# High and low activations side by side: 512-column matmuls in the weight-stationary products of a three-way split float32 decoder

## The chip, the cores and the metric

The kernel runs on one core of one Trainium2 chip. The time of a run is the device time of one execution in microseconds (us); the time before is the median of three runs. The profile is of one further execution, which has its own time. TensorE is PE in the profile (its weight loads are PEld), VectorE is DVE, ScalarE is ACT, GpSimd is POOL, SyncE is SP.

## The reference, cut to what matters

Four layers over 256 tokens of 1,024 features. Each layer has a mixer (layers 0 and 3 a convolution module, layer 1 a state-space mixer, layer 2 differential attention), then cross-attention to 256 memory tokens with 4 heads, then a gated feed-forward of inner width 2,816; each ends in a layer norm.

```
for i in range(DEPTH):
    y = conformer_conv(...) | ssd_mixer(...) | diff_attention(...)
    x = post_norm(x, y, ln_g[i, 0], ln_b[i, 0])
    x = post_norm(x, memory_cross_attention(x, mem, xa_w_q[i], xa_w_kv[i], xa_w_out[i]), ...)
    x = post_norm(x, swiglu(x, ff_w_in[i], ff_w_out[i]), ...)

def post_norm(x, y, g, b):
    return layer_norm(DN_ALPHA * x + y, g, b)

def swiglu(x, w_in, w_out):
    g, u = jnp.split(x @ w_in, 2, axis=-1)
    return (jax.nn.silu(g) * u) @ w_out
```

Everything is float32.

## The kernel before

**Split products.** Each float32 operand is held as a high part h (rounded to the type that TensorE multiplies) and a low part l, the rest. A product a·b is the sum of three matmuls into the same PSUM bank: ah·bh, ah·bl, al·bh (`mm3`, lines 199, 200 and 201).

**Weights.** `_Weights` streams blocks of 128 x 1024 numbers (512 KB) from HBM in a fixed plan: a DMA from SP's queue into one of four raw buffers, a cast on ACT to the high part `wh` (L152), two subtractions of 128x512 on DVE to the low part `wl` (L155). The pairs lie in a ring of seven; the block three ahead of the one taken is prepared when a block is taken. A cast into a ring place must wait until the block that lay there has been used.

**Activations.** `transpose_split` turns the 256 tokens into `XTh` and `XTl`, two tiles of 128 x 8 x 256 (eight k-tiles of features, 256 tokens); `MTh` and `MTl` are the same for the memory.

**The two forms of product.** In `gemm_a` and in the output products the weights are the moving operand, 512 columns per matmul. In `gemm_b_steps` the weights are stationary and the tokens move, 256 columns per matmul: for 256 output features (two halves j of 128) and 1,024 input features in two weight blocks b of four k-tiles,

```
for b in range(2):
    wh, wl = self.W.get(name, i, 4 * b, 4, *segs)
    for k in range(4):
        kk = 4 * b + k
        for j in range(2):
            self.mm3(ps[:, j, :], wh[:, k, js], wl[:, k, js], xh[:, kk, :], xl[:, kk, :], ...)
```

That is 24 matmuls of 256 columns per block and 48 per product. Both halves j share one PSUM bank. `gemm_b` serves three places: `ff`, the loop over feed-forward chunks 1 to 10 (a gate product and an up product in each); `q_part` in the cross-attention (heads 2 and 3); and the four K units per layer of `kv_unit`, which project the memory for the next cross-attention and are laid by `kv_unit` and its generator between other work.

**PSUM.** Eight banks: four for output sums (`pso`), two for the products above and other middle results (`psi`, taken in turn), two for transposes and scores (`psm`).

**A feed-forward chunk.** Gate product into one psi bank, tanh on ACT (L726), gate times sigmoid on DVE (L727, reads PSUM), up product into the other psi bank, product on DVE (L733, reads PSUM), split into `ch` and `cl` (L206, L210). Then two output blocks of 12 matmuls of 512 columns for the chunk before (L290, L291, L294). `out_tail` ends the layer with 48 output matmuls, the layer norm of both token halves (x0, x1; L334, L242, L341, L346) and the transposes into the next XT (L219), among which a K unit of the memory runs.

The order of instructions on each engine is set when the program is recorded; a scheduler in the recording layer places them by estimated readiness.

Of the kernel before, what the change touches and what calls it, by code (L numbers as in the profile page):

```python
# [26 lines left out]
D_FF = 2816  # L27
# [136 lines left out]
class _Trunk:  # L164
# [97 lines left out]
    def gemm_b(self, *args):  # L262
        for _ in self.gemm_b_steps(*args):
            pass

    def gemm_a(self, name, i, segs, done, which="o"):
# [50 lines left out]

    def new_xt(self, wanted=True):

        self.XTh = self.XTl = None  # L320
        if wanted:
            self.XTh = self.main.tile([P, KT, S], F32R, tag="XTh", name=self.uid("XTh"))
            self.XTl = self.main.tile([P, KT, S], F32R, tag="XTl", name=self.uid("XTl"))
# [31 lines left out]
    def setup(self):  # L355
        nc, ins = self.nc, self.ins
        self.x = [self.main.tile([P, D], F32, tag=f"x{t}", name=f"x{t}") for t in range(T)]
        self.alpha = ALPHA
        self.ident = self.const.tile([P, P], F32, name="ident")
        nc.vector.memset(self.ident, 1.0)  # L360
        nc.gpsimd.affine_select(
            out=self.ident, in_=self.ident, pattern=[[-1, P]], compare_op=ALU.is_equal, fill=0.0, base=0,
            channel_multiplier=1,
        )
        self.mhalf = self.const.tile([P, 8], F32, name="mhalf")
        nc.vector.memset(self.mhalf, -0.5)
        self.new_xt()
        self.MTh = self.main.tile([P, KT, S], F32R, name="MTh")
        self.MTl = self.main.tile([P, KT, S], F32R, name="MTl")
        self.memK = self.main.tile([P, KT, S], F32, name="memK")  # L370
        self.memVh = self.main.tile([P, T, D], F32R, name="memVh")
        self.memVl = self.main.tile([P, T, D], F32R, name="memVl")
        early = self.const.tile([P, 1], F32, name="early")
        nc.scalar.activation(out=early, in_=self.mhalf[:, 0:1], func=AF.Tanh)
        for t in range(T):
            for c in range(2):
                cs = slice(c * 512, (c + 1) * 512)
                nc.sync.dma_start(out=self.x[t][:, cs], in_=ins["x"][0][t * P : (t + 1) * P, cs])
            with self.tc.high_priority():
                self.transpose_split(self.x[t], self.XTh, self.XTl, t)  # L380
            if t == 0:
                self.W.prefetch(1)
# [8 lines left out]
    def kv_steps(self, layer):  # L391
# [3 lines left out]
        self.kv_next += 1  # L395
        i, u = divmod(u, 8)
        nc = self.nc
        ps = self.bank("i", a=2)
        if u < 4:
            yield from self.gemm_b_steps(ps, "xa_w_kv", i, ((u * 256, 256),), self.MTh, self.MTl)  # L400
            nc.scalar.copy(out=self.memK[:, 2 * u : 2 * u + 2, :], in_=ps)
            return
# [180 lines left out]
    def xattn(self, i):  # L583
        nc = self.nc
        ln = self.load_ln(i, 1)
        with self.stage_pool(f"xa{i}", 2) as wk:
# [17 lines left out]
                return (qh[:, 0:2, :], ql[:, 0:2, :]), (qh[:, 2:4, :], ql[:, 2:4, :])  # L604

            def q_part(h):
                ps = self.bank("i", a=2)
                self.gemm_b(ps, "xa_w_q", i, ((h * 256, 256),), self.XTh, self.XTl)
                qh, ql = parts(2, "xr")
                self.split(ps, qh, ql, 1.0 / 16.0)  # L610
                return qh, ql

            def s_part(h, q):
# [78 lines left out]
    def ff(self, i, nxt, hooks):  # L692
        nc = self.nc
        ln = self.load_ln(i, 2)
        with self.stage_pool(f"ff{i}", 2) as wk:
# [20 lines left out]
            for c in range(1, NFF):  # L716
                for step in hooks.get(c, ()):
                    step()
                psg = self.bank("i")
                psu = self.bank("i")  # L720
                self.gemm_b(
                    psg.rearrange("p (a b) -> p a b", a=2), "ff_w_in", i, ((c * 256, 256),), self.XTh, self.XTl
                )
                th = wk.tile([P, 512], F32, tag="fth", name=self.uid("fth"))
                sg = wk.tile([P, 512], F32, tag="fsg", name=self.uid("fsg"))
                nc.scalar.activation(out=th, in_=psg, func=AF.Tanh, scale=0.5)  # L726
                nc.vector.scalar_tensor_tensor(out=sg, in0=th, scalar=1.0, in1=psg, op0=ALU.add, op1=ALU.mult)  # L727
                self.gemm_b(
                    psu.rearrange("p (a b) -> p a b", a=2), "ff_w_in", i, ((D_FF + c * 256, 256),),
                    self.XTh, self.XTl,  # L730
                )
                h2 = wk.tile([P, 512], F32, tag="fh2", name=self.uid("fh2"))
# [673 lines left out]
```

## Time and profile before

| what | value |
|---|---|
| median of three runs | 1762.99 us (1761.61 to 1763.95) |
| profiled execution | 1762.06 us, its span 1760.3 us |
| granted TensorE clock, mean | 0.996 of full speed |
| PE busy | 1718.8 us, 98% of the span, 11,356 matmuls |
| PE weight loads | 1555.8 us, 88% |
| DVE busy | 1247.9 us, 71% |
| ACT busy | 844.6 us, 48% |
| DMA | 55.9% of 16 engines, 176 GB/s |

The span is the time from the first to the last instruction that the profile shows. Busy matmul time counts overlapping matmuls once; the duration of a single matmul (about 0.28 us for 256 columns) holds its pipeline, so what one costs in a row is the distance of starts.

### The profile page before, as it was taken

To read this page: it belongs to the slowest core of one execution; us is meant where nothing else is said; L and a number is where in the kernel's file an instruction comes from. 1 tells how busy PE (TensorE), PEld (TensorE's weight loads), DVE (VectorE), ACT (ScalarE), POOL (GpSimd) and SP (SyncE) were. 2 spreads that over 40 slices of the span, in tenths; PEclk is the share of its full clock that TensorE was granted. 3 is DMA by queue.
4 is the path that set the end of the run, shared out by engine and by line. 5 is a ranking of instruction groups with operands and counts; after the bars stand their busy time and mean duration, and the time that the engine had idled before them with its cause. 6 is when DMAs were issued, how large, how long until landed. Compare 5 with 4: busy or idle time off the path is not lost.

```text
span 1760.3 us, 29243 instructions
## 1 busy us (share of the span) xinstructions
PE 1718.8 (98%) x11356; PEld 1555.8 (88%) x11356; DVE 1247.9 (71%) x2306; ACT 844.6 (48%) x1250; POOL 55.6 (3%) x72
## 2 busy tenths in 40 slices
PE   7999999999999999999999999999999999999998
PEld 4887989999999998999998889889899888879997
DVE  4879675557898878675557677775555889775555
ACT  3445444444665654454444565544444445544442
POOL 0000000000011010000000000000000000000000
PEclk9999999999999999999999999999999999999999
DMA  7637465656656645465655643556565645556562
GB/s 229 210 115 224 148 198 185 187 185 183 202 169 179 179 157 167 138 211 184 191 181 183 188 132 120 181 155 207 170 187 183 217 139 170 190 169 189 182 190 72
DMA packets 234098, 310.05 MB, mean 176 GB/s; under 512 B 14104, under 2 KB 196774, under 8 KB 233960
## 3 DMA queue, kind: packets, MB, share of 16 engines
q1 hardware_dynamic: 233832, 307.90, 55.9%
q8 instruction: 89, 1.46, 0.3%
q14 instruction: 49, 0.40, 0.1%
q10 hardware_dynamic: 128, 0.29, 0.0%
HBM read 307.07 MB, written 1.08 MB: 175 GB/s over the span
## 4 chain that ended last, share of the span: by engine, by line
PE 72%; DVE 9%; DMA 5%; ACT 2%; issue 2%; SPq 0%; POOL 0%; DVEq 0%; ACTq 0%; POOLq 0%
PE psi L199 14%; PE psi L200 14%; PE psi L201 14%; PE pso L291 5%; PE pso L290 5%; PE pso L294 5%; DVE wl L155 3%; PE pso L199 2%; PE pso L201 2%; PE pso L200 2%; DMA raw<-in_xa_w_q 2%; ACT wh L152 1%; DVE st L242 1%; DVE x L334 1%; DVE x L346 1%
## 5 line engine op out<-in xcount | busy, mean ns | idle before, releaser
L155 DVE TENSOR_TENSOR wl<-raw,wh 128x512 fp32r<-128x512 f32 x1074 | 704.3, 686 | 396.8 <-ACT wh L152 394.5
L152 ACT CAST wh<-raw 128x1024 fp32r<-128x1024 f32 x537 | 560.3, 1048 | 686.6 <-PE psi L200 312.9
L199 PE MATMUL psi<-XTh,wh 128*128 128x256 f32 x1792 | 510.4, 285 | 0.2
L200 PE MATMUL psi<-XTl,wh 128*128 128x256 f32 x1792 | 507.9, 283 | 0.0
L201 PE MATMUL psi<-XTh,wl 128*128 128x256 f32 x1792 | 507.7, 283 | 0.0
L199 PEld LDWEIGHTS psi<-XTh,wh 128*128 128x128 f32 x1792 | 344.4, 192 | 3.9 <-issue 2.0
L200 PEld LDWEIGHTS psi<-XTl,wh 128*128 128x128 f32 x1792 | 344.5, 192 | 2.5 <-issue 0.8
L201 PEld LDWEIGHTS psi<-XTh,wl 128*128 128x128 f32 x1792 | 344.4, 192 | 0.0
L290 PE MATMUL pso<-wh,ch 128*128 128x512 f32 x448 | 176.1, 393 | 0.0
L291 PE MATMUL pso<-wl,ch 128*128 128x512 f32 x448 | 175.3, 391 | 0.0
L294 PE MATMUL pso<-wh,cl 128*128 128x512 f32 x448 | 139.4, 391 | 0.0
L294 PEld LDWEIGHTS pso<-wh,cl 128*128 128x128 f32 x448 | 84.1, 188 | 17.7
L291 PEld LDWEIGHTS pso<-wl,ch 128*128 128x128 f32 x448 | 84.4, 188 | 15.6
L290 PEld LDWEIGHTS pso<-wh,ch 128*128 128x128 f32 x448 | 84.4, 188 | 15.4 <-ACT ch L206 0.2
L199 PE MATMUL pso<-wh,XTh 128*128 128x512 f32 x224 | 89.5, 400 | 0.5 <-ACT XTh L206 0.4
L201 PE MATMUL pso<-wh,XTl 128*128 128x512 f32 x224 | 88.9, 397 | 0.3 <-DVE XTl L208 0.2
L200 PE MATMUL pso<-wl,XTh 128*128 128x512 f32 x224 | 87.7, 392 | 0.0
L234 POOL TENSOR_TENSOR rs<-rv,mhalf 128x1 f32<-128x1 f32 (+2 forms) x40 | 37.0, 924 | 1330.5 <-DVE rv L233 1330.5
L199 PE MATMUL pso<-wh,ch 128*128 128x512 f32 x192 | 76.0, 397 | 0.0
L201 PE MATMUL pso<-wh,cl 128*128 128x512 f32 x192 | 74.6, 392 | 0.0
L200 PE MATMUL pso<-wl,ch 128*128 128x512 f32 x192 | 74.4, 391 | 0.0
L199 PE MATMUL psi<-wh,MTh 128*128 128x256 f32 x256 | 73.6, 287 | 0.5 <-DVE memVl L208 0.4
(315 smaller groups left out, 2644.9 us busy)
## 6 DMA issues: line engine op xcount, KB each, us to landing
raw<-in_ff_w_in SPq DMA_DIRECT2D x160, 512.0 KB, 3.6
raw<-in_ff_w_out SPq DMA_DIRECT2D x88, 512.0 KB, 3.3
raw<-in_xa_w_kv SPq DMA_DIRECT2D x64, 512.0 KB, 3.5
raw<-in_cv_w_in SPq DMA_DIRECT2D x64, 256.0 KB, 4.8
raw<-in_xa_w_q SPq DMA_DIRECT2D x32, 512.0 KB, 3.5
raw<-in_xa_w_out SPq DMA_DIRECT2D x32, 512.0 KB, 4.7
raw<-in_mb_w_in SPq DMA_DIRECT2D x32, 512.0 KB, 4.0
raw<-in_da_w_qkv SPq DMA_DIRECT2D x24, 512.0 KB, 4.5
```

Source lines behind the costliest of these rows:

```text
L152: nc.scalar.copy(out=wh, in_=raw)
L155: nc.vector.tensor_tensor(out=wl[:, a : a + m], in0=raw[:, a : a + m], in1=wh[:, a : a + m].bitcast(F32), op=ALU.subtract)
L199: mm(out, ah, bh, start=start, stop=False)
L200: mm(out, ah, bl, start=False, stop=False)
L201: mm(out, al, bh, start=False, stop=stop)
L234: nc.gpsimd.tensor_tensor(out=r, in0=v, in1=self.mhalf[:, :cols], op=ALU.pow)
L242: nc.vector.bn_stats(out=st[:, h, :], in_=halves[h])
L290: mm(acc[t][c], hh[:, ts], wh[:, 0, cs], start=first, stop=False)
L291: mm(acc[t][c], hh[:, ts], wl[:, 0, cs], start=False, stop=False)
L294: mm(acc[t][c], hl[:, ts], wh[:, 0, cs], start=False, stop=last)
L334: nc.vector.scalar_tensor_tensor(out=x[:, cs], in0=x[:, cs], scalar=self.alpha, in1=acc[t][c], op0=ALU.mult, op1=ALU.add)
L346: nc.vector.scalar_tensor_tensor(out=x[:, cs], in0=x[:, cs], scalar=r, in1=b[:, cs], op0=ALU.mult, op1=ALU.add)
```

## The change

`XTh` and `XTl` become two halves of one tile `XT` with 512 columns per k-tile, and `MTh`, `MTl` halves of `MT`. A new `gemm_c_steps` takes the place of `gemm_b_steps` at its three places. It takes both weight blocks first, then goes half by half: for each half j a psi bank of its own, for each block four matmuls of `wh` by the 512 columns [Xh | Xl] over the whole bank, then four of `wl` by the 256 columns Xh added onto the bank's second half. When a half is done, ACT copies the bank's first half to SBUF and DVE adds the second half to it (`summed`). What followed reads SBUF instead of PSUM.

```
+    def gemm_c_steps(self, name, i, segs, X, done):
+        mm = self.nc.tensor.matmul
+        ws = [self.W.get(name, i, 4 * b, 4, *segs) for b in range(2)]
+        for j in range(2):
+            js = slice(j * P, (j + 1) * P)
+            ps = self.bank("i")
+            for b, (wh, wl) in enumerate(ws):
+                for k in range(4):
+                    mm(ps, wh[:, k, js], X[:, 4 * b + k, :], start=b == 0 and k == 0, stop=False)
+                for k in range(4):
+                    mm(ps[:, S : 2 * S], wl[:, k, js], X[:, 4 * b + k, 0:S], start=False, stop=b == 1 and k == 3)
+                if b == 1:
+                    done(j, ps[:, 0:S], ps[:, S : 2 * S])
+                yield
+    def summed(self, out):
+        def done(j, main, rest):
+            self.nc.scalar.copy(out=out[:, j, :], in_=main)
+            self.nc.vector.tensor_tensor(out=out[:, j, :], in0=out[:, j, :], in1=rest, op=ALU.add)
+        return done
...
 kv_unit, units 0 to 3:
-            yield from self.gemm_b_steps(ps, "xa_w_kv", i, ((u * 256, 256),), self.MTh, self.MTl)
-            nc.scalar.copy(out=self.memK[:, 2 * u : 2 * u + 2, :], in_=ps)
+            yield from self.gemm_c_steps(
+                "xa_w_kv", i, ((u * 256, 256),), self.MT, self.summed(self.memK[:, 2 * u : 2 * u + 2, :])
+            )
...
 q_part:
-                self.gemm_b(ps, "xa_w_q", i, ((h * 256, 256),), self.XTh, self.XTl)
+                self.gemm_c("xa_w_q", i, ((h * 256, 256),), self.XT, self.summed(nat))
-                self.split(ps, qh, ql, 1.0 / 16.0)
+                self.split(nat, qh, ql, 1.0 / 16.0)
...
 ff, chunks 1 to 10:
+                self.gemm_c("ff_w_in", i, ((c * 256, 256),), self.XT, self.summed(ga))
-                nc.scalar.activation(out=th, in_=psg, func=AF.Tanh, scale=0.5)
-                nc.vector.scalar_tensor_tensor(out=sg, in0=th, scalar=1.0, in1=psg, op0=ALU.add, op1=ALU.mult)
+                nc.scalar.activation(out=th, in_=ga, func=AF.Tanh, scale=0.5)
+                nc.vector.scalar_tensor_tensor(out=sg, in0=th, scalar=1.0, in1=ga, op0=ALU.add, op1=ALU.mult)
+                self.gemm_c("ff_w_in", i, ((D_FF + c * 256, 256),), self.XT, self.summed(h2))
-                nc.vector.tensor_tensor(out=h2, in0=sg, in1=psu, op=ALU.mult)
+                nc.vector.tensor_tensor(out=h2, in0=h2, in1=sg.rearrange("p a b -> p (a b)"), op=ALU.mult)
```

PE, the gate product of a feed-forward chunk in layer 1. Before, one block's first rows (moving operand named first, then the stationary one):

```order
L199 MATMUL psi_702_8685<-XTh_662_8242,wh231_8612 128x256
L200 MATMUL psi_702_8685<-XTl_663_8243,wh231_8612 128x256
L201 MATMUL psi_702_8685<-XTh_662_8242,wl231_8613 128x256
L199 MATMUL psi_702_8685<-XTh_662_8242,wh231_8612 128x256
L200 MATMUL psi_702_8685<-XTl_663_8243,wh231_8612 128x256
L201 MATMUL psi_702_8685<-XTh_662_8242,wl231_8613 128x256
```

Now, the whole gate product, both halves:

```order
L277 MATMUL psi_747_8314<-XT_703_7890,wh231_8213 128x512 x4
L279 MATMUL psi_747_8314<-XT_703_7890,wl231_8214 128x256 x4
L277 MATMUL psi_747_8314<-XT_703_7890,wh232_8263 128x512 x4
L279 MATMUL psi_747_8314<-XT_703_7890,wl232_8264 128x256 x4
L277 MATMUL psi_748_8333<-XT_703_7890,wh231_8213 128x512 x4
L279 MATMUL psi_748_8333<-XT_703_7890,wl231_8214 128x256 x4
L277 MATMUL psi_748_8333<-XT_703_7890,wh232_8263 128x512 x4
L279 MATMUL psi_748_8333<-XT_703_7890,wl232_8264 128x256 x4
```

A block's 24 matmuls have become 16, the two blocks alternate, and a product takes two psi banks one after the other.

ACT in the same chunk. Before, from the first cast of the chunk to the split of its result:

```order
L152 CAST wh236_8755<-raw236_8753 128x1024
L152 CAST wh237_8786<-raw237_8784 128x1024
L152 CAST wh238_8823<-raw238_8821 128x1024
L152 CAST wh239_8842<-raw239_8840 128x1024
L726 ACTIVATE fth_704_8749<-psi_702_8685 128x512
L152 CAST wh240_8870<-raw240_8868 128x1024
L152 CAST wh241_8901<-raw241_8899 128x1024
L206 ACTIVATE ch_707_8817<-fh2_706_8815 128x512
```

Now (fga holds the gate sum, fh2 the up sum):

```order
L152 CAST wh237_8366<-raw237_8364 128x1024
L292 COPY fga_746_8299<-psi_747_8314 128x256
L152 CAST wh238_8416<-raw238_8414 128x1024
L152 CAST wh239_8435<-raw239_8433 128x1024
L292 COPY fga_746_8299<-psi_748_8333 128x256
L755 ACTIVATE fth_749_8352<-fga_746_8299 128x512
L292 COPY fh2_751_8356<-psi_752_8371 128x256
L152 CAST wh240_8462<-raw240_8460 128x1024
L152 CAST wh241_8469<-raw241_8467 128x1024
L292 COPY fh2_751_8356<-psi_753_8390 128x256
L152 CAST wh242_8519<-raw242_8517 128x1024
L206 ACTIVATE ch_754_8410<-fh2_751_8356 128x512
```

Four copies stand among the casts, the second and the fourth behind two casts.

PE where layer 2's feed-forward ends: x0 and x1 are the token halves after the norm, psm their transposes, MT the memory, pso the last output sum. Before:

```order
L199 MATMUL pso_1078_12968<-wh414_14633,ch_1147_14521 128x512
L200 MATMUL pso_1078_12968<-wl414_14634,ch_1147_14521 128x512
L201 MATMUL pso_1078_12968<-wh414_14633,cl_1148_14522 128x512
L219 MATMUL psm_1162_14768<-ident_93,x0_91 128x128 x4
L219 MATMUL psm_1163_14776<-ident_93,x0_91 128x128 x4
L199 MATMUL pso_1078_12968<-wh415_14664,ch_1154_14695 128x512
L200 MATMUL pso_1078_12968<-wl415_14665,ch_1154_14695 128x512
```

Now:

```order
L201 MATMUL pso_1154_12322<-wh416_13845,cl_1261_13840 128x512
L277 MATMUL psi_1275_13997<-MT_99,wh417_13852 128x512
L219 MATMUL psm_1267_13911<-ident_93,x0_91 128x128 x4
L277 MATMUL psi_1275_13997<-MT_99,wh417_13852 128x512
L219 MATMUL psm_1268_13919<-ident_93,x0_91 128x128 x4
L277 MATMUL psi_1275_13997<-MT_99,wh417_13852 128x512 x2
L279 MATMUL psi_1275_13997<-MT_99,wl417_13853 128x256 x4
...
L279 MATMUL psi_1276_14016<-MT_99,wl418_13860 128x256 x4
L219 MATMUL psm_1273_13964<-ident_93,x1_92 128x128 x4
L219 MATMUL psm_1274_13972<-ident_93,x1_92 128x128 x4
```

The transposes of x0 have moved behind all 48 output matmuls, and those of x1 stand directly behind the K unit.

## Rows read from the trace of the kernel before

**Rows 1.** The profile page: busy time of each engine, the clock over 40 slices of the span (tenths of full speed), and the shares of the chain of work that ended last.

```profile
PE 1718.8 (98%) x11356; PEld 1555.8 (88%) x11356; DVE 1247.9 (71%) x2306; ACT 844.6 (48%) x1250; POOL 55.6 (3%) x72
...
PEclk9999999999999999999999999999999999999999
...
PE 72%; DVE 9%; DMA 5%; ACT 2%; issue 2%; SPq 0%; POOL 0%; DVEq 0%; ACTq 0%; POOLq 0%
```

**Rows 2.** PE's waits over the whole span: what waited, for what, us in total, times, longest.

```profile
PE psm L219 <- DMA x<-in_x: 7.0, 2, 4.8
PE psm L599 <- ACT xnat L596: 5.9, 4, 1.9
PE psi L199 <- ACT XTh L206: 4.9, 1, 4.9
PE psm L219 <- DVE x L346: 3.5, 3, 1.7
PE psm L831 <- DVE sd_dta L826: 1.6, 1, 1.6
```

**Rows 3.** Busy time of each engine in one feed-forward chunk of layer 1 (gate and up products, then two output blocks): the stretch, its length, then busy us and instructions of PE, PEld, DVE, ACT and POOL, the clock, the DMA share and GB/s.

```profile
804.27:821.25 16.98, 16.98 (x122) 16.02 (x120) 9.65 (x15) 7.32 (x8) 0.00 (x0) 1.00 0.59 189
```

**Rows 4.** Timeline of PE: start, duration, line, operands. First the ends of the 96 matmuls of 256 columns of that chunk and the 24 of 512 columns behind them; last the first and the last of 27 matmuls of 512 columns in a row at the end of layer 2.

```profile
804.27 0.28 PE L199 MATMUL psi<-XTh,wh 128*128 128x256 f32 x1
...
815.78 0.40 PE L290 MATMUL pso<-wh,ch 128*128 128x512 f32 x1
...
817.17 0.39 PE L290 MATMUL pso<-wh,ch 128*128 128x512 f32 x1
...
821.25 0.28 PE L199 MATMUL psi<-XTh,wh 128*128 128x256 f32 x1
...
1362.97 0.39 PE L199 MATMUL pso<-wh,ch 128*128 128x512 f32 x1
...
1368.86 0.39 PE L201 MATMUL pso<-wh,cl 128*128 128x512 f32 x1
```

**Rows 5.** Groups of ACT instructions that follow the three uses of the old product, one per gate product, per product of `q_part`, per K unit: out<-in, shapes, count, busy us, mean ns, and the idle time before them.

```profile
L726 ACT ACTIVATE fth<-psi 128x512 f32<-128x512 f32 x40 | 23.8, 594 | 1.9 <-PE psi L201 1.9
L206 ACT ACTIVATE xrh<-psi 128x512 fp32r<-128x512 f32 x8 | 4.7, 593 | 0.0
L401 ACT COPY memK<-psi 128x512 f32<-128x512 f32 x16 | 9.2, 578 | 12.2 <-PE psi L201 12.2
```

**Rows 6.** Groups of instructions on ACT and DVE, same columns: a 128x256 copy out of PSUM, a 128x256 operation of two tensors that reads PSUM, the cast and the subtraction of a weight block.

```profile
L1205 ACT COPY dpT<-psm 128x256 f32<-128x256 f32 x8 | 3.0, 376 | 0.8 <-PE psm L1203 0.8
L948 DVE TENSOR_TENSOR xdt<-psm,sd_dt 128x256 f32<-128x256 f32 x16 | 6.0, 414 | 0.0
L152 ACT CAST wh<-raw 128x1024 fp32r<-128x1024 f32 x537 | 560.3, 1048 | 686.6 <-PE psi L200 312.9 <-issue 132.6 <-PE pso L294 85.8
L155 DVE TENSOR_TENSOR wl<-raw,wh 128x512 fp32r<-128x512 f32 x1074 | 704.3, 686 | 396.8 <-ACT wh L152 394.5 <-issue 0.2
```

**Rows 7.** Timeline of ACT in that chunk; in brackets the idle time before and what ended it.

```profile
807.26 1.05 ACT L152 CAST wh<-raw 128x1024 fp32r<-128x1024 f32 x1 [1.71 <-PE psi L200]
810.14 1.05 ACT L152 CAST wh<-raw 128x1024 fp32r<-128x1024 f32 x1 [1.83 <-PE psi L200]
```

**Rows 8.** Timeline of DVE in that chunk.

```profile
808.35 1.29 DVE L155 TENSOR_TENSOR wl<-raw,wh 128x512 fp32r<-128x512 f32 x2 [1.46 <-ACT wh L152]
...
815.98 0.69 DVE L733 TENSOR_TENSOR fh<-fsg,psi 128x512 f32<-128x512 f32 x1 [0.59 <-PE psi L201]
```

**Rows 9.** The end of layer 2's feed-forward: timeline of DVE (the norm of x0, and the last step of x1's norm) and of PE (transposes of x0, first matmul of the K unit, transposes of x1), and busy times over the K unit.

```profile
1363.17 0.69 DVE L334 SCALAR_TENSOR_TENSOR x<-x,pso 128x512 f32<-128x512 f32 x1 [0.80 <-PE pso L201]
...
1368.30 1.41 DVE L346 SCALAR_TENSOR_TENSOR x<-x,rs,lnb 128x512 f32<-128x512 f32 x2
...
1377.07 1.40 DVE L346 SCALAR_TENSOR_TENSOR x<-x,rs,lnb 128x512 f32<-128x512 f32 x2
...
1369.10 1.32 PE L219 MATMUL psm<-ident,x 128*128 128x128 f32 x8
...
1371.64 0.28 PE L199 MATMUL psi<-MTh,wh 128*128 128x256 f32 x1
...
1378.32 0.60 PE L219 MATMUL psm<-ident,x 128*128 128x128 f32 x4
...
1371.64:1377.51 5.87, 5.87 (x50) 5.86 (x49) 5.87 (x12) 1.87 (x2) 0.93 (x1) 1.00 0.33 104
```

**Rows 10.** Layer 0's cross-attention: the last matmul of head 0's output product on PE, and the two instructions that empty its psi bank, on ACT and on DVE.

```profile
188.90 0.28 PE L201 MATMUL psi<-xpTh,memVl 128*128 128x256 f32 x1
...
189.22 0.60 ACT L206 ACTIVATE ch<-psi 128x512 fp32r<-128x512 f32 x1 [0.19 <-PE psi L201]
...
189.85 0.69 DVE L208 TENSOR_TENSOR cl<-psi,ch 128x512 fp32r<-128x512 f32 x1
```

**Rows 11.** Layer 2's differential attention: the first and last instructions that empty the psi bank with four heads' outputs, on ACT and on DVE.

```profile
1066.90 0.29 ACT L1212 ACTIVATE don<-psi 128x128 f32<-128x128 f32 x1
...
1070.37 0.33 DVE L1215 SCALAR_TENSOR_TENSOR don<-psi,rs,da_sg 128x128 f32<-128x128 f32 x1
```

More of the change, by code (lines that the diff above doesn't have):

```diff
@@ L264, in gemm_b, with gemm_c @@
             pass
+    def gemm_c_steps(self, name, i, segs, X, done):
[12 more added lines that the diff above has]
+                yield
+    def gemm_c(self, *args):
+        for _ in self.gemm_c_steps(*args):
+            pass
+    def summed(self, out):
[3 more added lines that the diff above has]
+        return done
     def gemm_a(self, name, i, segs, done, which="o"):
@@ L318, in new_xt @@
     def new_xt(self, wanted=True):
-        self.XTh = self.XTl = None
+        self.XT = self.XTh = self.XTl = None
         if wanted:
-            self.XTh = self.main.tile([P, KT, S], F32R, tag="XTh", name=self.uid("XTh"))
-            self.XTl = self.main.tile([P, KT, S], F32R, tag="XTl", name=self.uid("XTl"))
+            self.XT = self.main.tile([P, KT, 2 * S], F32R, tag="XT", name=self.uid("XT"))
+            self.XTh, self.XTl = self.XT[:, :, 0:S], self.XT[:, :, S : 2 * S]
     def load_ln(self, i, s):
@@ L367, in setup @@
         self.new_xt()
-        self.MTh = self.main.tile([P, KT, S], F32R, name="MTh")
-        self.MTl = self.main.tile([P, KT, S], F32R, name="MTl")
+        self.MT = self.main.tile([P, KT, 2 * S], F32R, name="MT")
+        self.MTh, self.MTl = self.MT[:, :, 0:S], self.MT[:, :, S : 2 * S]
         self.memK = self.main.tile([P, KT, S], F32, name="memK")
@@ L397, in kv_steps @@
         nc = self.nc
+        if u < 4:
+            yield from self.gemm_c_steps(
+                "xa_w_kv", i, ((u * 256, 256),), self.MT, self.summed(self.memK[:, 2 * u : 2 * u + 2, :])
+            )
+            return
         ps = self.bank("i", a=2)
-        if u < 4:
-            yield from self.gemm_b_steps(ps, "xa_w_kv", i, ((u * 256, 256),), self.MTh, self.MTl)
-            nc.scalar.copy(out=self.memK[:, 2 * u : 2 * u + 2, :], in_=ps)
-            return
         for b in range(2):
@@ L606, in q_part @@
             def q_part(h):
-                ps = self.bank("i", a=2)
-                self.gemm_b(ps, "xa_w_q", i, ((h * 256, 256),), self.XTh, self.XTl)
+                nat = wk.tile([P, 2, S], F32, tag="xnat", name=self.uid("xnat"))
+                self.gemm_c("xa_w_q", i, ((h * 256, 256),), self.XT, self.summed(nat))
                 qh, ql = parts(2, "xr")
-                self.split(ps, qh, ql, 1.0 / 16.0)
+                self.split(nat, qh, ql, 1.0 / 16.0)
                 return qh, ql
@@ L718, in ff @@
                     step()
[L719 to L725, printed above, removed]
-                nc.scalar.activation(out=th, in_=psg, func=AF.Tanh, scale=0.5)
-                nc.vector.scalar_tensor_tensor(out=sg, in0=th, scalar=1.0, in1=psg, op0=ALU.add, op1=ALU.mult)
[L728 to L732, printed above, removed]
-                nc.vector.tensor_tensor(out=h2, in0=sg, in1=psu, op=ALU.mult)
+                ga = wk.tile([P, 2, S], F32, tag="fga", name=self.uid("fga"), bufs=1)
+                self.gemm_c("ff_w_in", i, ((c * 256, 256),), self.XT, self.summed(ga))
+                th = wk.tile([P, 2, S], F32, tag="fth", name=self.uid("fth"))
+                sg = wk.tile([P, 2, S], F32, tag="fsg", name=self.uid("fsg"))
+                nc.scalar.activation(out=th, in_=ga, func=AF.Tanh, scale=0.5)
+                nc.vector.scalar_tensor_tensor(out=sg, in0=th, scalar=1.0, in1=ga, op0=ALU.add, op1=ALU.mult)
+                h2 = wk.tile([P, 2, S], F32, tag="fh2", name=self.uid("fh2"))
+                self.gemm_c("ff_w_in", i, ((D_FF + c * 256, 256),), self.XT, self.summed(h2))
+                h2 = h2.rearrange("p a b -> p (a b)")
+                nc.vector.tensor_tensor(out=h2, in0=h2, in1=sg.rearrange("p a b -> p (a b)"), op=ALU.mult)
                 ch = self.chunk.tile([P, 512], F32R, tag="ch", name=self.uid("ch"))
```

## The prediction

> **What bounds the kernel now.** First the page's busy times and chain [rows 1]: PE is busy for 1718.8 of 1760.3 us, it stands for 72% of the chain that ended last, and its clock stays at nine tenths or more in all 40 slices. Then PE's waits [rows 2]: the largest are 7.0, 5.9 and 4.9 us, at the start and in the cross-attention. Feeding PE better has little left to give, so what shortens the kernel is fewer or shorter matmuls, and what lengthens it is a new wait of PE. Then one feed-forward chunk [rows 3]: in its 16.98 us PE is busy throughout, DVE for 9.65 and ACT for 7.32, at full clock. Last the starts on PE's timeline [rows 4]: 96 matmuls of 256 columns take 815.78 − 804.27 = 11.51 us, 0.1199 each, and 18 of 512 columns from 817.17 to 821.25 take 4.08, 0.2267 each. So doubling the columns costs 0.1068 us, and about 13 ns of each matmul do not depend on its columns. That is what the change can remove.
>
> **What is removed.** A block goes from 24 matmuls of 256 columns to 8 of 512 and 8 of 256; the columns stay 6,144. By those two spacings it goes from 24 × 119.9 = 2,878 ns to 8 × 226.7 + 8 × 119.9 = 2,773 ns: 105 ns less. Matmuls of 512 columns that add into the same bank one after another, as now, have a row too: 26 spacings from 1362.97 to 1368.86, 0.2265 each [rows 4]. The number of blocks comes from what follows each product [rows 5]: 40 tanh, so 80 gate and up products; 8 splits of q; 16 copies of K. That is 104 products of two blocks, 208 blocks: **−21.8 us**, of which the feed-forward has 16.8, K 3.4 and q 1.7.
>
> The Trainium skill, page "TensorE: Matmul & The Clock Gate", section "Back-to-back issue gap", gives the gap of isolated matmuls at full clock as N/2.4 + 2.5 ns, which leaves only 2.5 ns per matmul removed. By it the sum of this part would be 8 × 2.5 × 208 = 4.2 us, an estimate from that page; the spacings measured here disagree (0.2267 and 0.1199 against its 0.2158 and 0.1092), and I go by them.
>
> **What reading PSUM costs PE.** The first six 512-column matmuls of an output block, during which DVE reads PSUM (L733 at 815.98 [rows 8]), take 817.17 − 815.78 = 1.39 us, 0.2317 each against 0.2267 [rows 4]: 5 ns more. The change adds reads: for each half a copy on ACT and an add on DVE. Their nearest rows are 0.376 and 0.414 us [rows 6], so 1.6 us per product, some two thirds of it under 512-column matmuls: about 4.6 matmuls × 5 ns × 104 = 2.4 us. Bounds: 0 (the difference may be chance) and 5 (all that PE does is slowed). I take **+2.4**.
>
> **The emptying itself.** 208 copies × 0.376 = 78 us on ACT less 16 old copies of K (9.2 us [rows 5]), and 208 adds × 0.414 = 86 us on DVE. In a feed-forward chunk, now 16.98 − 0.42 = 16.56 us long, DVE goes from 9.65 to 11.3 and ACT from 7.32 to 8.8: neither becomes the bound, and their cover is PE's own work. What could stop PE is when a bank comes free. A gate or up product took one bank, which was needed again 5.7 us after it was full; now each half takes one and its bank is needed after 4 × (4 × 0.2267 + 4 × 0.1199)/2 = 2.77 us. The tight one is the second half of the gate: in ACT's order its copy stands behind two casts, and the second of these waits for the ring place of the gate's own second block. That place's high part is free 0.48 us (four matmuls by wl) before the half is full; call that moment of fullness E. Cast from E − 0.23 to E + 0.82 (0.25 for the release, 1.05 for the cast [rows 6, 7]), copy to E + 1.21; DVE by then does the first subtraction of that cast until E + 1.5, then the add until E + 1.9. Needed at E + 2.77: 0.8 us to spare. The second half of the up product has 1.7 by the same count. Result: **0** in the loop; the bounds of this term are 0 and, if the add comes a whole cast and subtraction pair later (1.05 + 1.29 us), 1.5 us × 40 chunks; I take 0 because the worked moment is far nearer to the lower end.
>
> **Layer ends.** In three layers the order of PE changes (the third place of the section on the change). Before, x0's chain on DVE ran from 1363.17 to L346 at 1368.30, x0's transposes began at 1369.10, the K unit ran from 1371.64, and x1's transposes were at 1378.32, behind L346 at 1377.07 [rows 9]; DVE was busy without a gap over the K unit (5.87 of 5.87 us). Now the first output sum is done eight matmuls later in PE's order but for the four that the second loses: the release for x0's norm moves by about 4 × 0.227 = 0.91 us. PE reaches x1's transposes 1.1 to 1.7 us earlier, since the four convolution matmuls ahead of them are gone and the K unit is 0.2 shorter, while DVE's chain for x1 is three subtractions shorter but starts 0.91 later and takes in an operation of x1 ahead: some 0.5 later or earlier than PE. I take 0.7 us of wait in each, **+2**, bounds 0 and 2.1 each (0 to 6.3), the upper being the whole lead of PE plus the 0.91 that stays.
>
> **Cross-attention.** `q_part` for head 3 now needs both psi banks. The second is the bank of head 0's output product, emptied by ACT at 189.22 and DVE at 189.85 to 190.54, 1.6 us after the last matmul at 188.90 began [rows 10]; a little over 2.4 us lie between that product and the first use, and the new copies and adds of q stand in the same queues: +0.4. Head 3's split then starts from an SBUF copy, one copy and one add later (0.8 us); in PE's order head 2's scores and head 1's output product stand between, and hold most of that. For four layers I take **+2**, bounds 0 and 6.
>
> **Differential attention.** The K units there lie between heads, and in one place the second half of a unit, and behind it the heads' output, take a bank whose emptying runs from 1066.90 to 1070.70 [rows 11]: about 3.8 us, against 2.5 that the new order leaves. **+1**, bounds 0 and 3.
>
> **The sum.** −21.8 + 2.4 + 0 + 2 + 2 + 1 = −14.4. Against the profiled execution's own 1762.06 us (span 1760.3) that is 1747.7; the median of the runs lies 0.9 above the profiled one, so the forecast is **1748.6 us**.
>
> **Rivals.**
> - *Nothing is given back.* PE meets all banks in time and the reads of PSUM cost nothing: −18 to −22, about 1742. For it: the waits of before are tiny [rows 2], and a stall at layer 1's start (L831, 1.6 us) could vanish in the new order. Against it: DVE without a gap at the layer ends [rows 9].
> - *More is given back* at layer ends, cross-attention and differential attention: all upper bounds of these (6.3 + 6 + 3) and 5 for PSUM are 20.3, so −1.5; the middle of this case is −6, 1757.
> - *Slower: the second gate half is emptied too late.* If the copy and add end later than E + 2.77, PE stops in each of the 40 chunks. The spare time is 0.8 us; the rest of the sum is −14.4, so the change turns to a loss when a chunk waits more than 0.36 us, that is when the release is 1.2 us later than worked. For it: three queues (PE to ACT's cast, ACT's copy, DVE's add) must each pass in turn behind a cast or a subtraction of 1.05 and 1.29 us; a whole pair later would be (2.34 − 0.8) × 40 = 62 us, and the first cast of the pair alone, (1.05 − 0.8) × 40 = 10 us. Against it: ACT idles 1.7 us before each cast today [rows 7] and DVE 1.4 before each pair [rows 8]. At half a microsecond per chunk the time would be 1748 + 20 = 1768.
> - *The columns set the time, not the count.* If 512 columns in this form take twice 0.1199, 8 × 0.2398 + 8 × 0.1199 is the old block, and the emptying is pure loss: 0 + 7.4, about 1770. Against it stand two rows of 512-column matmuls at 0.2267 and 0.2265 [rows 4].
>
> The page's formula named above would be a milder form of this: a gain of 4.2 us, eaten by the same 7.4.
>
> **How the numbers follow.** A measurement of this kernel tells 0.2%, 3.5 us, from no change: faster is below 1759.5, slower above 1766.5. Chances: the main case (−8 to −18) 0.60; nothing given back 0.17; more given back 0.12, of which a third ends within 0.2%; slower by the gate's bank 0.08, a quarter of it within 0.2%; columns alone 0.03. Faster 0.85, same 0.06, slower 0.09. The likeliest case's own range is 1744 to 1755. For eight in ten I go from 1740, the whole gain with nothing back and a little for stalls that vanish, to 1759, the middle of "more given back" and a little over.
>
> **What will show it.** Spacing on PE in a chunk: 0.227 for L277 and 0.120 for L279, a chunk of 16.5 to 16.6 us with no wait in it, and some 1,660 matmuls fewer. Copies (L292) near 0.38 and adds (L293) near 0.42 us. In PE's waits: new rows for psi against the copies or the adds of `summed`, under 1 us per layer in the feed-forward; x1's transposes waiting for L346 (now L377) up to 1 us in three layers; one wait of `q_part` per layer. The prediction is wrong if L277 waits for the add in every chunk, if 512-column matmuls on the joined tile are spaced above 0.232, or if the layer ends cost more than 2 us each.

## The result and the profile after

The changed kernel takes 1752.28 us in the median of four runs (1750.39 to 1753.31), the kernel before 1762.85 beside it: 0.9929 of it, 95% interval 0.9913 to 0.9946. A second series gave 0.9954 (0.9935 to 0.9972). The profiled execution's span is 1749.7 us, 10.6 less than before. The forecast was 1748.6 in a range of 1740 to 1759, faster. Of all executions in this document one, of the split kernel below, took 2400.24 us at a granted clock of 0.655; it counts in that kernel's median and not in its ratio.

The page of after, busy times (before: [rows 1]):

```profile
span 1749.7 us, 26246 instructions
...
PE 1705.1 (97%) x9692; PEld 1466.5 (84%) x9692; DVE 1324.2 (76%) x2514; ACT 912.6 (52%) x1442; POOL 57.1 (3%) x72
```

PE has 1,664 matmuls fewer and 13.7 us less busy time; DVE has 76 us more and ACT 68 more, none of it on PE's path in the loop. One feed-forward chunk of layer 1, with the columns of [rows 3]:

```profile
795.88:812.57 16.69, 16.69 (x89) 14.31 (x88) 11.17 (x20) 8.77 (x12) 0.00 (x0) 1.00 0.63 190
```

It was 16.98 us [rows 3] and was forecast at 16.5 to 16.6; the 16.62 that an expectation below names ends 0.07 us before the next chunk begins. PE's timeline in it (xN joins N matmuls, so the distance of starts is what N of them take):

```profile
795.88 1.07 PE L277 MATMUL psi<-XT,wh 128*128 128x512 f32 x4
796.79 0.64 PE L279 MATMUL psi<-XT,wl 128*128 128x256 f32 x4
797.26 1.09 PE L277 MATMUL psi<-XT,wh 128*128 128x512 f32 x4
798.19 0.63 PE L279 MATMUL psi<-XT,wl 128*128 128x256 f32 x4
798.66 1.09 PE L277 MATMUL psi<-XT,wh 128*128 128x512 f32 x4
799.59 0.64 PE L279 MATMUL psi<-XT,wl 128*128 128x256 f32 x4
```

The first four matmuls of 512 columns, behind an output block, take 0.91 us, 0.227 each as in [rows 4]. The next groups, behind 256-column matmuls, take 0.93. That is the first surprise. PE's largest waits (before: [rows 2]):

```profile
PE psm L219 <- DMA x<-in_x: 6.7, 2, 4.6
PE psi L199 <- ACT XT L206: 4.9, 1, 4.9
PE psm L631 <- ACT xnat L628: 3.4, 2, 1.8
PE psm L598 <- DVE cv_u L595: 3.3, 1, 3.3
PE psi L199 <- DVE memK L293: 2.7, 1, 2.7
PE psm L199 <- DVE cvp L541: 2.7, 1, 2.7
```

L277 has no row in the whole list: no joined product waited for a bank. The waits for `cv_u` and `memK` are new. The third new thing is the clock. PE stands at the lower level, 1.2 GHz, for 6.82 us from 1449.02, which begins within the wait for `cv_u` (PE idle until 1450.00), and for as long from 1247.63. Before, there was no such stretch at the former place, and one of 3.41 us, from 1261.71, at the latter; PE had no wait there, but ran eight matmuls of only 31 rows (`taps`), from 1244.69 after the change and from 1257.21 before:

```profile
1247.63:1254.45 6.82, 6.82 (x17) 4.01 (x17) 2.02 (x4) 0.00 (x0) 0.00 (x0) 0.50 0.46 153
1449.02:1455.84 6.82, 5.84 (x28) 5.80 (x29) 6.82 (x15) 4.06 (x8) 0.00 (x0) 0.50 0.56 180
```

```profile
1261.71:1265.12 3.41, 3.41 (x16) 3.36 (x16) 0.69 (x1) 0.00 (x0) 0.00 (x0) 0.50 0.65 204
```

**Where the time went.** All distances between the starts of neighbouring matmuls on PE, in the two profiled executions, sorted: each is its form's own time (0.2267 us for 512 columns, 0.1199 for 256, 0.109 for 128) plus an excess. Excess in stretches at the lower clock stands apart; elsewhere an excess above 0.06 us counts as a wait (this holds some slow forms that are the same in both), a smaller one as spacing. In us:

| part | before | after | difference |
|---|---|---|---|
| own time of all matmuls | 1684.2 | 1662.4 | −21.8 |
| spacing excess, 512 columns | 4.8 | 13.4 | +8.6 |
| spacing excess, 256 columns | −1.2 | −3.5 | −2.3 |
| spacing excess, 128 columns | −16.7 | −16.8 | −0.1 |
| waits | 71.5 | 73.1 | +1.6 |
| excess at the lower clock | 4.7 | 8.3 | +3.6 |
| first to last start on PE | 1747.3 | 1736.9 | −10.4 |

(The parts add up within their rounding.) Of the excess at the lower clock, about 2.7 us after the change lie in the stretch from 1449.02 and 3.7 in that from 1247.63 (1.6 at that place before); a stretch of 3.41 us from 67.05, worth 1.5, was there before only. This term differs between executions: the second profile of the changed kernel has two such stretches more, from 66.07 and 1369.96.

So there are three questions: whether the number of matmuls is what gave the gain, what made the 512-column matmuls 8.6 us slower, and where the waits come from.

### The profile page after: what moved, and what is told of

Read it like the earlier page. It is cut to its first block, busy times and chain, and to the rows that moved or that the text cites. A ratio compares the mean times of both kernels' runs of the same rounds, so it can differ in the third digit from the quotient of the medians.

```text
span 1749.7 us, 26246 instructions
## 1 busy us (share of the span) xinstructions
PE 1705.1 (97%) x9692; PEld 1466.5 (84%) x9692; DVE 1324.2 (76%) x2514; ACT 912.6 (52%) x1442; POOL 57.1 (3%) x72
## 4 chain that ended last, share of the span: by engine, by line
PE 81%; DVE 5%; DMA 2%; ACT 1%; issue 1%; POOL 0%; SPq 0%; DVEq 0%; ACTq 0%; POOLq 0%
PE psi L277 20%; PE psi L279 10%; PE pso L321 6%; PE pso L322 6%; PE pso L325 6%; PE psi L199 5%; PE psi L200 5%; PE psi L201 5%; PE pso L199 4%; PE pso L201 4%; PE pso L200 4%; DVE wl L155 1%; PE psm L219 1%; DVE st L242 1%; DMA raw<-in_xa_w_q 1%
## 5 line engine op out<-in xcount | busy, mean ns | idle before, releaser
L277 PE MATMUL psi<-XT,wh 128*128 128x512 f32 x1408 | 387.1, 396 | 0.0
L277 PEld LDWEIGHTS psi<-XT,wh 128*128 128x128 f32 x1408 | 243.6, 189 | 36.7 <-issue 2.4
L279 PEld LDWEIGHTS psi<-XT,wl 128*128 128x128 f32 x1408 | 216.5, 189 | 29.9
L279 PE MATMUL psi<-XT,wl 128*128 128x256 f32 x1408 | 224.4, 281 | 0.0
L322 PE MATMUL pso<-wl,ch 128*128 128x512 f32 x448 | 175.4, 392 | 0.0
L199 PE MATMUL psi<-XT,wh 128*128 128x256 f32 x384 | 111.3, 290 | 0.0
L201 PE MATMUL psi<-XT,wl 128*128 128x256 f32 x384 | 108.7, 283 | 0.0
L200 PE MATMUL psi<-XT,wh 128*128 128x256 f32 x384 | 108.6, 283 | 0.0
L321 PEld LDWEIGHTS pso<-wh,ch 128*128 128x128 f32 x448 | 84.1, 188 | 16.6 <-ACT ch L206 0.9
L199 PE MATMUL pso<-wh,XT 128*128 128x512 f32 x224 | 89.2, 399 | 0.1
L201 PE MATMUL pso<-wh,XT 128*128 128x512 f32 x224 | 88.4, 395 | 0.3 <-DVE XT L208 0.3
L200 PE MATMUL pso<-wl,XT 128*128 128x512 f32 x224 | 87.8, 392 | 0.0
L199 PE MATMUL psi<-wh,MT 128*128 128x256 f32 x256 | 74.6, 291 | 0.4 <-DVE memVl L208 0.4
```

Source lines behind the costliest of these rows:

```text
L199: mm(out, ah, bh, start=start, stop=False)
L200: mm(out, ah, bl, start=False, stop=False)
L201: mm(out, al, bh, start=False, stop=stop)
L277: mm(ps, wh[:, k, js], X[:, 4 * b + k, :], start=b == 0 and k == 0, stop=False)
L279: mm(ps[:, S : 2 * S], wl[:, k, js], X[:, 4 * b + k, 0:S], start=False, stop=b == 1 and k == 3)
L321: mm(acc[t][c], hh[:, ts], wh[:, 0, cs], start=first, stop=False)
```

## Experiments

Each is the changed kernel with the edit named. Times are compared by the ratio to the kernel before in the same series; "excess" and "waits" are parts of the table above, taken in the same way.

### Is it the number of matmuls?

```
-                    mm(ps, wh[:, k, js], X[:, 4 * b + k, :], ...)
+                    mm(ps[:, 0:S], wh[:, k, js], X[:, 4 * b + k, 0:S], ...)
+                    mm(ps[:, S : 2 * S], wh[:, k, js], X[:, 4 * b + k, S : 2 * S], ...)
```

> The changed kernel with the same banks, emptying and order of halves, but each matmul of 512 columns by wh is made of two of 256 (high activations to the bank's first half, low to its second): 24 matmuls per block again. Theory (the gain is the number of matmuls alone): in the changed kernel's trace a product takes 5.608 us on PE, with 48 matmuls at 0.1199 it takes 5.755, so 104 x 0.147 = 15.3 us longer than the changed kernel, about 1767 us, 4 to 5 above the kernel before, which is what the emptying, the layer ends and the clock cost. Rival (the gain comes from the order of halves or from reading SBUF in place of PSUM): within 3 us of the changed kernel's 1752.

Measured 1767.84 us, ratio 1.0043 (1.0030 to 1.0057); span 1764.2, 14.5 above the changed kernel's, 15.3 expected. Its waits stand at the same places as in the changed kernel:

```profile
PE psm L599 <- DVE cv_u L596: 3.3, 1, 3.3
PE psi L199 <- DVE memK L294: 2.7, 1, 2.7
```

and its spacing excess is that of before (512: 4.8, 256: −0.8). So the count of matmuls gives the gain; halves, banks and emptying without it make the kernel slower than before.

### What slows the 512-column matmuls?

In the feed-forward, the copies and adds read `x`, a tile in SBUF, so that the gate and up products are left out of the result:

```
-            self.nc.scalar.copy(out=out[:, j, :], in_=main)
-            self.nc.vector.tensor_tensor(out=out[:, j, :], in0=out[:, j, :], in1=rest, op=ALU.add)
+            self.nc.scalar.copy(out=out[:, j, :], in_=x)
+            self.nc.vector.tensor_tensor(out=out[:, j, :], in0=out[:, j, :], in1=x, op=ALU.add)
```

> In the feed-forward the copies and adds read a tile in SBUF in place of the PSUM bank (so gate and up products do not enter the result); all else as in the changed kernel. Theory P, of the prediction (DVE and ACT reading PSUM slow the 512-column matmuls): the groups of four 512-column matmuls in a chunk go back from 929 to 907 ns. Theory T (a loss at each passage from 256 to 512 columns, whatever the other engines do): the second group of each half stays at 233, 236, 228, 232 and the chunk within 0.05 us of the changed kernel's 16.62.

One execution, 1742.43 us beside a median of 1761.19. PE's timeline in a chunk:

```profile
794.16 1.09 PE L277 MATMUL psi<-XT,wh 128*128 128x512 f32 x4
795.09 0.63 PE L279 MATMUL psi<-XT,wl 128*128 128x256 f32 x4
795.56 1.09 PE L277 MATMUL psi<-XT,wh 128*128 128x512 f32 x4
796.49 0.64 PE L279 MATMUL psi<-XT,wl 128*128 128x256 f32 x4
```

Still 0.93 for four, the chunk from one gate product to the next is 16.69 us in both kernels, and over the whole span the 512s have 13.2 us of excess against 13.4. The reading of PSUM does not slow them: theory P of the prediction falls. (That this run is shorter lies in 4.1 us less of waits and 5.0 less at the lower clock; without a bank to wait for, its instructions were laid in another order.)

All 512s of a half first:

```
             for b, (wh, wl) in enumerate(ws):
                 for k in range(4):
                     mm(ps, wh[:, k, js], X[:, 4 * b + k, :], start=b == 0 and k == 0, stop=False)
+            yield
+            for b, (wh, wl) in enumerate(ws):
                 for k in range(4):
                     mm(ps[:, S : 2 * S], wl[:, k, js], X[:, 4 * b + k, 0:S], start=False, stop=b == 1 and k == 3)
...
```

> The changed kernel with one edit: per half first all eight matmuls of 512 columns of both blocks, then all eight of 256. In the changed kernel's trace each group of four 512-column matmuls behind 256-column ones is 22 ns too long (234, 234, 232, 228 against 227), the groups behind output blocks are not. Theory A (a fixed loss per passage from 256 to 512 columns): half as many passages, 22 x 208 = 4.6 us less, 1748. Theory B (the loss goes on for some eight matmuls after a passage, as in the output blocks, 42 ns over eight): 8 matmuls lose 42 ns once in place of 22 twice, no change, 1751 to 1753.

Measured 1744.09, ratio 0.9912 (0.9894 to 0.9930); once more beside the changed kernel on another chip:

> All 512s of a half first, once more, beside the changed kernel on the same chip. If the loss per passage is real it is 0.1 to 0.3% faster than the changed kernel; if the first result came from the chip or from the clock, the two are within 0.1%.

> The changed kernel itself, to stand beside the others of this call on one chip: 0.991 to 0.995 of the kernel before.

1748.92, 0.9932 (0.9914 to 0.9951), against 1754.09, 0.9954 (0.9935 to 0.9972). Both times 0.2% better than the changed kernel, though the intervals overlap. The trace is clearer. PE's timeline:

```profile
799.70 1.98 PE L277 MATMUL psi<-XT,wh 128*128 128x512 f32 x8
801.51 1.11 PE L281 MATMUL psi<-XT,wl 128*128 128x256 f32 x8
802.46 2.00 PE L277 MATMUL psi<-XT,wh 128*128 128x512 f32 x8
804.30 1.12 PE L281 MATMUL psi<-XT,wl 128*128 128x256 f32 x8
805.25 1.09 PE L277 MATMUL psi<-XT,wh 128*128 128x512 f32 x4
```

The eight behind an output block take 1.81 us, the eight behind 256s 1.84. The single spacings behind a 256 are 233, 236, 228, 232, 231 ns, then 227: five matmuls lose 26 ns together, and the loss does not depend on how many follow. The first two 256s behind a 512 take 113 and 119 instead of 120, 7 ns back. Excess of the 512s over the span 9.4 and 9.5 us against 13.4, of the 256s −2.6 against −3.5: 3 us gained, and the chunk is 16.61 us. Theory A holds in kind; its 4.6 us were too many, since the longer run loses 26 ns and not 22 and the 256s give less back.

wl and wh alternating:

```
                 for k in range(4):
                     mm(ps, wh[:, k, js], X[:, 4 * b + k, :], start=b == 0 and k == 0, stop=False)
-                for k in range(4):
                     mm(ps[:, S : 2 * S], wl[:, k, js], X[:, 4 * b + k, 0:S], start=False, stop=b == 1 and k == 3)
```

> The changed kernel with each half's 512- and 256-column matmuls alternating, wh then wl for each k-tile, so every 512 stands behind a 256: eight passages per half in place of two. In the trace with all 512s of a half first, a passage lengthens the five 512s behind it by 6, 9, 1, 5 and 4 ns and shortens the first 256 after by 7. Theory T1 (the loss belongs to the 512s that follow within some five matmuls of a 256): about 6 ns at each 512, 6 x 8 = 48 per half where the changed kernel has 44: no more than 2 us slower than the changed kernel. Theory T2 (a fixed 20 to 25 ns for each passage): 8 x 20 = 160 ns per half, 208 x 0.12 = 24 us slower.

One execution, 1760.24 us beside a median of 1761.19; 512s at 20.2 us of excess, 256s at −6.0: 4.3 us net above the changed kernel, between the 2 of T1 and the 24 of T2, far nearer to T1. A single 512 behind a 256 takes 236 ns here and the 256 behind it 117 (medians). So the loss belongs to the 512s within some five matmuls behind a 256. (The rest of its 8.7 us is 3.9 at the lower clock and 0.7 of waits.)

The second half running the other way:

```
+            wide, low = [(1, k) for k in range(KT)], [(0, k) for k in range(KT)]
+            steps = wide + low if j == 0 else wide[:1] + low + wide[1:]
...
```

> As the run with both edits, but the second half goes the other way: one 512 (which opens the bank), then its eight 256s, then its other seven 512s, so that the next product's or output block's 512s follow on 512s. Passages from 256 to 512 per product: two, one of them for a single 512, and none ahead of the output blocks, in place of two and one. If a passage loses 19 to 26 ns: 104 x 16 + 40 x 26 ns = 2.7 us less than the run with both edits, 0.15%; if the loss is of another kind, no difference or slower by the longer wait for the low parts of the weights.

1749.98, 0.9937 (0.9919 to 0.9956): not faster than 0.9908 (0.9892 to 0.9924) without this edit, rather slower. Spacing improved by 0.7 us only (512s 7.9, 256s −1.7), since the 256s gave back less, and the waits rose by 4.1 us. A miss.

### Where do the new waits come from?

The end of layer 2 in the changed kernel, on DVE and on PE (before: [rows 9]):

```profile
1363.69 1.42 DVE L377 SCALAR_TENSOR_TENSOR x<-x,rs,lnb 128x512 f32<-128x512 f32 x2
1365.02 1.30 DVE L155 TENSOR_TENSOR wl<-raw,wh 128x512 fp32r<-128x512 f32 x2
1366.22 1.29 DVE L208 TENSOR_TENSOR XT<-psm,XT 128x512 fp32r<-128x512 f32 x2
1367.41 0.69 DVE L155 TENSOR_TENSOR wl<-raw,wh 128x512 fp32r<-128x512 f32 x1
1368.01 0.76 DVE L293 TENSOR_TENSOR memK<-memK,psi 128x256 f32<-128x256 f32 x2
```

```profile
1364.59 1.29 PE L219 MATMUL psm<-ident,x 128*128 128x128 f32 x8
1368.59 0.47 PE L199 MATMUL psi<-wh,XT 128*128 128x512 f32 x1 [2.71 <-DVE memK L293]
```

x1's transposes came at 1364.59 without a wait. But the two adds that free the K unit's banks stand in DVE's order behind x1's norm, three subtractions and two splits; ACT had copied the first half at 1361.85. The next layer's first product waits 2.71 us for them. To test whether the adds are to blame: the K units as before, and, second, the adds recorded at high priority (the diffs in this order):

> The changed kernel with the K units of the memory as before (48 matmuls of 256 columns, one copy from one bank); feed-forward and q_part changed. Theory (the adds of the K units stand on DVE behind the norms, so PE waits for the bank: 2.7 us at 1366 and a part of the 3.4 us at 1446 in the changed kernel, after which the clock is at half for 6.8 us): the 16 units lose 2.4 us of gain and 5 to 8 us of waits and clock go: 1747 to 1750. Rival (these waits come from how the scheduler laid the new lengths, whatever empties the K units): 1752 to 1756.

> The changed kernel with the copies and adds that empty the banks recorded at high priority, so that in DVE's order they stand ahead of norms and subtractions. Theory (late adds of the K units): no wait for a memK add on PE, the 2.7 us at the end of layer 2 and part of the 3.4 in layer 3's convolution gone, 1746 to 1750. Rival (the scheduler's new lengths, not the place of the adds): 1751 to 1756.

```
-            yield from self.gemm_c_steps(
-                "xa_w_kv", i, ((u * 256, 256),), self.MT, self.summed(self.memK[:, 2 * u : 2 * u + 2, :])
-            )
+            yield from self.gemm_b_steps(ps, "xa_w_kv", i, ((u * 256, 256),), self.MTh, self.MTl)
+            nc.scalar.copy(out=self.memK[:, 2 * u : 2 * u + 2, :], in_=ps)
...
```

```
+            with self.tc.high_priority():
                 self.nc.scalar.copy(out=out[:, j, :], in_=main)
                 self.nc.vector.tensor_tensor(out=out[:, j, :], in0=out[:, j, :], in1=rest, op=ALU.add)
```

The first: 1751.30, 0.9946 (0.9929 to 0.9963). The second: 1744.48, 0.9911 (0.9894 to 0.9928). PE's waits from the end of layer 2 through layer 3's convolution (1340 to 1460), first the changed kernel, then high priority:

```profile
PE psm L598 <- DVE cv_u L595: 3.3, 1, 3.3
PE psi L199 <- DVE memK L293: 2.7, 1, 2.7
PE psm L598 <- DVE rv L233: 0.9, 1, 0.9
PE pso L321 <- ACT ch L206: 0.5, 1, 0.5
```

```profile
PE psm L199 <- DVE cvp L542: 3.2, 1, 3.2
PE psi L199 <- DVE cva L519: 0.8, 1, 0.8
```

In this stretch both edits remove the waits for `memK` and for `cv_u`, but another, for `cvp`, comes in (3.2 and 2.8 us); elsewhere high priority has three waits for `memK` of 0.4 to 0.7 us. Over the span, waits fall by 4.8 us with high priority and by 3.7 with the old K units, which give back 3.3 of own time. So the K units' form is worth nothing with late adds.

How an add comes into the wait for `cv_u` shows at the last K unit of layer 3's convolution, on ACT, DVE and PE of the changed kernel, and last on DVE of the run with all 512s of a half first:

```profile
1436.75 0.36 ACT L292 COPY memK<-psi 128x256 f32<-128x256 f32 x1
```

```profile
1449.17 0.69 DVE L595 SCALAR_TENSOR_TENSOR cv_u<-clt,cv_u 128x512 f32<-128x512 f32 x1
1449.77 0.42 DVE L293 TENSOR_TENSOR memK<-memK,psi 128x256 f32<-128x256 f32 x1
```

```profile
1450.00 1.09 PE L598 MATMUL psm<-ident,cv_u 128*128 128x128 f32 x4 [3.28 <-DVE cv_u L595]
1450.74 0.56 PE L199 MATMUL psi<-wh,MT 128*128 128x256 f32 x1
```

```profile
1437.59 0.42 DVE L294 TENSOR_TENSOR memK<-memK,psi 128x256 f32<-128x256 f32 x1 [0.42 <-ACT memK L293]
```

The add stands behind L595, so the wait does not end on it. But the add frees the bank of the next product of the memory, and it comes 13.0 us behind ACT's copy. In PE's order that product stands at 1450.74, behind the third group of transposes of `cv_u`, and PE has no other work under the convolution's norm. With the add at 1437.59 the product's matmuls lie between the transposes. That the late add is what moved the product back is inferred, since the order was set before the run; the other traces agree with it. In six (the changed kernel twice, the split matmuls, the reads of SBUF, the alternating order and the run with the old feed-forward below) the add comes 12.0 to 13.0 us behind the copy, and the wait is 3.3 in each. In six (all 512s first, twice; high priority; the run with the second half reversed; the two of the last section below) it comes 0.4 us behind, and the wait is 0.3 or gone.

So late adds are the cause of these two waits, for `memK` by the rows and for `cv_u` by the twelve traces. But high priority is not the only thing that moves them: all 512s first did so with the adds recorded as in the changed kernel (0.2 us for `memK` and 0.3 for `cv_u` in this stretch). Why the scheduler lays them late in one order and early in another is not tested, nor why the wait for `cvp` comes with the new order of the convolution.

The feed-forward as before, K units and `q_part` changed (of two products, the gate's):

```
-                self.gemm_c("ff_w_in", i, ((c * 256, 256),), self.XT, self.summed(ga))
+                self.gemm_b(
+                    psg.rearrange("p (a b) -> p a b", a=2), "ff_w_in", i, ((c * 256, 256),), self.XTh, self.XTl
+                )
```

> Only the K units and q_part changed, the feed-forward's gate and up products as before (48 matmuls of 256 columns into one bank). By the changed kernel's spacings 24 of 104 products gain 0.147 us: 3.5 us. Theory (the emptying costs PE time at the K units, not in the feed-forward loop): the late adds stay and eat most of this, within 0.2% of the kernel before, 1759 to 1764 where that takes 1762, and the feed-forward alone is worth 8 to 12 us. Rival (waits come from the feed-forward's emptying): 4 us or more faster than the kernel before.

1761.65 beside 1761.58, 1.0009 (0.9992 to 1.0025), as the theory has it: no gain. Own time and spacing are some 4 us less than before, but the profile has the 3.3 us wait for `cv_u` again, and 3.0 us more at the lower clock. The wait for `memK` is not in it: at the end of layer 2 the two adds stand directly behind x1's norm (1374.29).

### Both improvements

All 512s of a half first, as in the diff above, with the emptying at high priority everywhere, and then in the K units alone:

> Two edits together: all eight 512s of a half first, and copies and adds at high priority. Each alone gave 0.9912 and 0.9911 of the kernel before. In the decomposition of the traces the first takes 3 us from the matmul spacings, the second 4.8 from the waits; if they are independent of each other the two give 0.9929 - 0.0017 - 0.0024, about 0.989, 1743 where the kernel before takes 1762. Rival (the scheduler's orders differ by as much by chance): 0.991 or above.

> All 512s of a half first, and copies and adds of the K units alone at high priority: those of the feed-forward and of q as the scheduler lays them. If only the K units' adds were late, as good as the version with every copy and add at high priority: 0.989 to 0.992.

The first gave 1745.11, 0.9908 (0.9892 to 0.9924): hardly better than either edit alone. The second, with high priority in the K units alone, 1741.64, 0.9890 (0.9871 to 0.9910), beside 0.9954 (0.9935 to 0.9972) for the changed kernel and 0.9932 (0.9914 to 0.9951) for all 512s first alone, in the same series: 0.6% faster than the changed kernel and 1.1% than before. Its profile has 9.4 us of excess at the 512s, 3.0 us less of waits and 1.9 less at the lower clock than the changed kernel's. The two versions' orders agree on PE and differ by one row on DVE and one on ACT, so their difference of 0.2% is more likely the chip or the run than the edit; differences of this size between series show nothing by themselves.

## Why the prediction was right, and which steps were off

- **Matmuls removed: right.** −21.8 us was forecast from the two spacings; the own time in the table falls by that, and splitting the 512s again takes 14.5 us of span back.
- **Reading PSUM: right sign, wrong cause, wrong size.** The step that failed is the reading of the six 0.2317 us matmuls at 815.78 [rows 4, 8]: DVE's read of PSUM lay beside them, and I took the company for the cause. They stood behind 256-column matmuls, and that is what lengthens them: in the kernel before, the first four 512s of an output block already take 233, 236, 228 and 233 ns (medians). Priced by the time of reads it was +2.4. Counted by passages, four per product less the one that follows an output block, some 376 × 22 ns = 8.3 us; measured +8.6 at the 512s and −2.3 at the 256s, +6.3.
- **Emptying in the loop at 0: right.** The chunk's DVE and ACT came to 11.17 and 8.77 us (11.3 and 8.8 forecast). The gate's second half was full at about 801.5 by the start of the next product; its add ended at 803.32 and the bank was wanted at 804.28, 0.96 us later (0.8 forecast):

```profile
802.90 0.42 DVE L293 TENSOR_TENSOR fga<-fga,psi 128x256 f32<-128x256 f32 x1
```

```profile
804.28 0.40 PE L277 MATMUL psi<-XT,wh 128*128 128x512 f32 x1
```

- **Copies and adds: right.** 369 and 418 ns, forecast 376 and 414.
- **Layer ends: size about right, place wrong.** x1's transposes, priced at 0.7 in each of three layers, waited for nothing at these three ends. (The rows of `x` in the lists, 3.5 us before and 1.2 after, lie at other norms: 154.42, 1489.84 and 1567.65 before, 151.35 and 1560.57 after.) The wait came one step later, at the bank of the K unit, whose add stands behind the norm on DVE: 2.7 us once, and 1.1 for the split of XT at layer 0's end, 3.8 in all against +2. The step that was left out is the place of the new DVE instruction in DVE's own order; the order of the changed kernel showed it.
- **Cross-attention: wrong sign.** +2 was forecast. `q_part` never waited, the wait on `xnat` (heads 0 and 1) fell from 5.9 to 3.4 and the waits for `xpTh` (0.7 us in four before) are gone from the list.
- **Differential attention: right.** +1 forecast; PE waits 0.8 for `don`, the heads' output of [rows 11], and 0.9 for `dp` behind it.
- **All waits together:** +5 forecast, +1.6 measured, as new waits and waits that went nearly cancel. The largest new one, 3.3 us for `cv_u` in layer 3's convolution, had no term at all. **Clock:** 0 forecast, +3.6 measured; 6.8 us at 1.2 GHz went with that wait, 6.8 more began at 1247.63, and no term of the sum allowed for either. The row that was read for it [rows 1] has slices of 44 us, in which the three stretches of 3.41 us of the kernel before do not show.
- **Its own signs of being wrong:** one stood at its limit and one came true. Four 512s behind 256s are spaced 0.232 on average, just at the limit of 0.232, and one layer end cost 2.7 us, above the limit of 2. No L277 waited for an add.

The misses of +3.9 (spacing), +3.6 (clock) and −3.4 (waits) make up, within 0.3 us, the 3.8 by which the span's difference fell short of −14.4. That the forecast came so near is in part luck: two terms that were too small were offset by one too large. The formula of the Trainium skill (page "TensorE: Matmul & The Clock Gate", section "Back-to-back issue gap") would have given a gain of 4.2 us before any cost, an estimate from that page; the trace disagrees, with 21.8 us less of own time.

## What to carry to other kernels

Where PE is busy all the time, join matmuls that share their stationary operand: here each one removed was worth 13 ns, 21.8 us in all, and in the feed-forward the emptying of the joined banks stayed behind PE. Keep runs of one width together: the passages between widths took 6.3 us back, and about half of that with all 512s of a half first. And when a change adds an instruction that frees a bank, look up what stands ahead of it in its own engine's order at the ends of the stages, not only its duration in the loop.

## What the runs showed of the hardware that was not expected

- Matmuls of 512 columns directly behind ones of 256 start 233, 236, 228, 232 and 231 ns apart instead of 227, also where the copies and adds of the feed-forward read SBUF in place of PSUM; behind eight 512s the first 256s take 113 and 119 ns instead of 120. What in TensorE does this stays open.
- The granted clock of one kernel differs from run to run, and its time with it: the kernel before gave 0.993 to 0.997 and 1756 to 1765 us in one series. In that series the lower clocks go with the longer times (correlation of the two −0.71; −0.22 and −0.81 in two other series), so a part of the scatter goes with this clock. A wait of some microseconds can cost about as much again at the clock: half of the 5.84 us that PE was busy in the stretch from 1449.02, an estimate of 2.9 us, beside the wait of 3.3. It does not do so each time: in the six traces with this wait, 6.8 us at 1.2 GHz begin in its last 2 us in four and 3.4 in two; behind the wait of 2.7 in layer 2 there is none in one profile of the changed kernel and 3.4 us in the other.
